# S5 mixer start-up: the scan's tables crossed over two PSUM banks, powers as three rows, x by channel half, and another order of GpSimd's work

## The chip, the cores and the metric

One core of a Trainium2 chip runs the whole program: a two-layer network on one sequence of 256 tokens, width 2048, in fp32. The metric is the device time of one execution in microseconds (us). The engines are TensorE (PE, matmuls and transposes through the identity), VectorE (DVE), ScalarE (ACT), GpSimd (POOL) and SyncE (SP, which here only issues DMAs). Each has its own instruction queue and runs it in order; between engines, and where one instruction of an engine needs an earlier one of the same engine, semaphores are waited on. PSUM, where PE writes its results, has eight banks of 512 fp32 values a partition.

## The reference, cut to what matters

Layer 0 is a mixer of diagonal state-space models ("S5"): 128 groups of 16 channels, 64 complex states a group. The state follows h[t] = lam * h[t-1] + B u[t], with lam = exp(dt * (a_re + i a_im)), and the output is Re(C h) plus a skip term, then gelu and a gated projection (GLU) with residual. Then comes a SwiGLU block, then layer 1 (dilated attention over three groups) and a second SwiGLU block. Cut to the mixer:

```
dt = exp(log_dt);  lb = exp(min(a_re, -1e-4)*dt) * (cos(a_im*dt) + i sin(a_im*dt))
coef = (lb - 1) / a;           bb = coef * b
bu = einsum('blgh,gph->blgp', u, bb)             # complex: _re and _im apart
st[t] = lb * st[t-1] + bu[t]                     # associative_scan in chunks of 128
y = einsum('blgp,ghp->blgh', st_re, c_re) - einsum('blgp,ghp->blgh', st_im, c_im) + d_skip*u
g = gelu(y);  val, gate = split(g @ w_glu);  x = x + val * sigmoid(gate)
```

## The kernel before, in words

The mixer does not scan 256 tokens. It takes four tokens as one step (so 64 steps, NS): the input of one step is the four tokens' inputs weighted with lam^3, lam^2, lam and 1 ("taps"), the step's factor is lam^4, and the outputs inside a step come from C lam^t ("fds", `powers`) and a small matrix over the four tokens ("mt", `build_m`). The 128 groups lie as 2 x 64 in partitions, and four quarters `qr` of 16 columns; a quarter has one chain of 63 steps.

All mixer work is issued through `InOrder` wrappers (T, A, G, W for PE, ACT, POOL, DVE), so that each engine's order is the order of the program text from line 547 on. The steps the change and the prediction touch:

- Lines 213-233: x as `xc` (two loads of 1 MB, on ACT's queue), `spp` (the state's parameters), `pairs`, `gb` and `bt` (gain and B), `ct` (C) on SP's.
- Lines 278-329: DVE computes `lam` from `spp` in about fifty instructions of 64 elements. ACT sums squares of x, PE adds them over partitions and repeats `NW` matmuls to keep its clock up, POOL takes the root, ACT scales x (`scale_x`).
- `form` and `power` (344-365): each power of lam is laid out as a 2x2 table of (re, im) factors in PSUM by four copies on DVE; ACT keeps the tables in SBUF as `pf` (`keep`). lam^4 is `tb3`, in a bank of its own; it holds the factors of all four chains (`fsc`), and the products of all four (`prs`) share the bank of table 2 (`tb2`).
- `gain` puts gain times B into `gps[qr]`; `taps(qr)` multiplies it by the powers (two products and an add for each of three taps). Quarters 0 to 2 are on DVE, 3 on POOL.
- `build_u(h)`: 32 transposes of x on PE, eight masked evictions by ACT. `taps_T(i)` transposes four columns' taps, `inject(i)` makes sixteen passes of matmul of them with x, and ACT copies the result into the state array `sts`; four injections make a quarter.
- `scan(qr)`: a generator of three DVE instructions a step: the product of the factor table with the state (128x64, into PSUM), and two adds into the next state (128x32). `run` takes one instruction of each generator in turn; `steps(n, a, b)` runs n steps of two chains.
- `build_c`, `powers` on POOL (chunks of two products and an add). `build_m`: ACT masks C, PE multiplies, ACT copies, SP moves copies by DMA. `y_local` and `y_state(qr, .., c0, c1)`: the outputs on PE, the state's part in halves of 32 steps. `gelu` on ACT, `turn` and `low` split the result into high and low fp32r halves as the left operand of the GLU.
- From line 679: 28 slots (`feed`) of twelve 128x512 matmuls, the first half of the GLU's depth, with chains 2 and 3 between them on DVE: a slot's DVE work is one `wlo` subtraction (the weights' low half) and two, two or three steps of both chains (`BSTEPS`). At slot 25 the last steps and `y_state(2)`, `y_state(3)` follow. The rest of the network begins after these slots.

Of the kernel before, what the change touches and what calls it, by code (L numbers as in the profile page):

```python
# [12 lines left out]
FP32 = mybir.dt.float32  # L13
# [3 lines left out]
ALU = mybir.AluOpType  # L17
# [30 lines left out]
NW = 14  # L48
# [14 lines left out]
class Net:  # L63
# [141 lines left out]
    def s5_glu(self):  # L205
# [110 lines left out]
        lam = early.tile([P, 2, 64], FP32, name="lam")  # L316
# [14 lines left out]
        tb0 = self.ps_mm.tile([P, 2, 2, 2, 64], FP32, name="mm")  # L331
        gpa = self.ps_mm.tile([P, 2, 16, GI], FP32, name="mm")
        tb2 = self.ps_mm.tile([P, 512], FP32, name="mm")
        tb3 = self.ps_mm.tile([P, 2, 2, 64], FP32, name="mm")
        half = lambda t, m: t.rearrange("p (k r m) -> p k r m", k=2, r=2)
        tabs = [tb0[:, 0], tb0[:, 1], half(tb2[:, 0:256], 64), tb3]
        prs = [half(tb2[:, 256 + 64 * k:320 + 64 * k], 16) for k in range(4)]
        fsc = [tb3[:, :, :, 16 * k:16 * k + 16] for k in range(4)]
        gpb = early.tile([P, 2, 16, GI], FP32, name="gpb")
        gqt = late.tile([P, 2, 2, 16, GI], FP32, name="gq", tag="gm", bufs=2)  # L340
        gq = [gqt[:, k] for k in range(2)]
        pf = late.tile([P, 4, 2, 2, 64], FP32, name="pf")
# [8 lines left out]
        def keep(t0, t1):
            for t in range(t0, t1):
                A.copy(out=pf[:, t].rearrange("p k r m -> p r k m"), in_=tabs[t])

        form(0, lam)
        pw = [lam]

        def power():
            k = len(pw)
            z = early.tile([P, 2, 64], FP32, name=f"pw{k}")  # L360
            pr = early.tile([P, 2, 2, 64], FP32, name="pr")
            tt(pr, tabs[0], pw[-1].unsqueeze(1).broadcast_to([P, 2, 2, 64]), ALU.mult, W)
            tt(z, pr[:, :, 0], pr[:, :, 1], ALU.add, W)
            pw.append(z)
            form(k, z)

        cf = late.tile([P, 2, 2, 64], FP32, name="cform")

        def coefs():
            ni = lam[:, 1]  # L370
            stt(t1, lam[:, 0], -1.0, ca, ALU.add, ALU.mult)
            tt(t2, ni, cb_, ALU.mult)
            stt(t3, lam[:, 0], -1.0, cb_, ALU.add, ALU.mult)
            tt(t4, ni, ca, ALU.mult)
            tt(cf[:, 0, 0], t1, t2, ALU.add)
            tt(cf[:, 0, 1], t3, t4, ALU.subtract)
            ts(cf[:, 1, 1], cf[:, 0, 0], -1.0, None, ALU.mult)
            V.tensor_copy(out=cf[:, 1, 0], in_=cf[:, 0, 1])
# [682 lines left out]
```

## Time and profile before

| what | us |
|---|---|
| median of three runs | 2454.3 (2450.5 to 2454.6) |
| profiled execution, its own time | 2451.0 |
| its span | 2449.2 |
| PE busy / DVE busy / ACT busy / POOL busy in the span | 2385.8 / 1377.0 / 1088.8 / 122.7 |
| first GLU matmul | 121.58 |
| second half of `y_state(2)` | 216.81 |

The span runs from the first to the last instruction. Busy times are sums of instruction lengths and overlap between engines. In a timeline row stand the start, the length, the engine (SPq or ACTq is a DMA issue), the line, the operation and its tiles as output<-inputs, with buffer numbers left out: in the mixer every instruction shows L60, the line of the recording wrapper, so they are told apart by tile and shape. `mm`, `tr` and `ms` are PSUM tiles, `actr` is any of the large SBUF tiles (x, the transposed x, the states, the mt matrices), `gp` a quarter's taps, `gt` their transposes, `fpr`, `cp` and `fdx` POOL's products, C and its powers.

### The profile page before, as it was taken

What the parts mean: (1) busy time and instruction counts of PE and PEld (TensorE: products, weight loads), DVE (VectorE), ACT (ScalarE), POOL (GpSimd) and SP (SyncE); (2) the same over time, 40 slices, a digit from 0 to 9 for tenths busy, and PEclk for the clock granted to TensorE, in tenths of its full rate; (3) what the DMA queues carried; (4) which work ended last, traced back from release to release, by engine and by line L of the source; (5) the groups of instructions that cost most, each with busy time, mean ns of one, the idle gap of its engine ahead of it and who ended that gap; (6) DMA issues with size and microseconds to landing.
All of it is one profiled execution on the core that took longest, in us unless ns stands there. A gap on an engine that the chain in (4) does not pass through costs nothing.

```text
span 2449.2 us, 29727 instructions
## 1 busy us (share of the span) xinstructions
PE 2385.8 (97%) x11856; PEld 1925.3 (79%) x11856; DVE 1377.0 (56%) x2309; ACT 1088.8 (44%) x1384; POOL 122.7 (5%) x105
## 2 busy tenths in 40 slices
PE   5689999999999999999999999999999999999999
PEld 4667887888888888888888888888878888888887
DVE  8897654544444445555546766775454444454444
ACT  6343554444334444454445555554443433344433
POOL 7600000000000000000000000000000000000000
PEclk8899999999999999999999999999999999999999
DMA  2244555555555555555554444445555555555554
GB/s 84 79 160 138 181 180 189 178 185 187 189 189 186 178 187 189 173 198 180 181 189 172 155 155 155 155 155 176 185 189 182 180 187 189 189 183 180 187 198 146
DMA packets 63036, 423.61 MB, mean 173 GB/s; under 512 B 8112, under 2 KB 9520, under 8 KB 12336
## 3 DMA queue, kind: packets, MB, share of 16 engines
q1 hardware_dynamic: 61456, 417.50, 49.9%
q10 hardware_dynamic: 1440, 4.19, 0.4%
q8 instruction: 93, 1.52, 0.2%
q14 instruction: 47, 0.39, 0.0%
HBM read 418.79 MB, written 2.10 MB: 172 GB/s over the span
## 4 chain that ended last, share of the span: by engine, by line
PE 91%; DVE 8%; issue 1%; ACT 0%; DMA 0%; DVEq 0%
PE mm L123 29%; PE mm L124 29%; PE mm L125 29%; DVE mm L60 3%; DVE actr L60 2%; DVE wlo L60 1%; PE ms L898 1%; PE tr L778 1%; PE tr L849 1%; PE tr L898 0%; PE tr L186 0%; PE tr L60 0%; PE mm L60 0%; DVE gp L60 0%; PE ms L60 0%
## 5 line engine op out<-in xcount | busy, mean ns | idle before, releaser
L105 DVE TENSOR_TENSOR wlo<-raw,whi 128x1024 fp32r<-128x1024 f32 x756 | 924.3, 1224 | 967.2 <-ACT whi L104 965.8
L104 ACT CAST whi<-raw 128x1024 fp32r<-128x1024 f32 x756 | 792.8, 1049 | 1125.7 <-PE mm L125 1102.0
L123 PE MATMUL mm<-whi,actt 128*128 128x512 f32 x3008 | 1196.8, 398 | 0.0
L124 PE MATMUL mm<-wlo,actt 128*128 128x512 f32 x3008 | 1190.9, 396 | 0.0
L125 PE MATMUL mm<-whi,actt 128*128 128x512 f32 x3008 | 1190.8, 396 | 0.0
L125 PEld LDWEIGHTS mm<-whi,actt 128*128 128x128 f32 x3008 | 564.7, 188 | 135.1
L123 PEld LDWEIGHTS mm<-whi,actt 128*128 128x128 f32 x3008 | 564.7, 188 | 132.9
L124 PEld LDWEIGHTS mm<-wlo,actt 128*128 128x128 f32 x3008 | 564.7, 188 | 132.5
L60 DVE TENSOR_TENSOR actr<-actr,mm 128x32 f32<-128x32 f32 x504 | 64.6, 184 | 8.0 <-ACT actr L60 3.5
L60 DVE TENSOR_TENSOR mm<-mm,actr 128x64 f32<-128x64 f32 x252 | 58.3, 231 | 8.1 <-ACT pf L60 0.4
L175 POOL TENSOR_TENSOR r<-m,mhalf 128x1 f32<-128x1 f32 x6 | 3.2, 552 | 1084.2 <-DVE m L174 846.7
L829 POOL TENSOR_TENSOR sc<-ssq,mhalf 128x8 f32<-128x8 f32 x16 | 32.1, 2004 | 474.9 <-DVE ssq L827 474.9
L60 ACT CAST whi<-raw 128x1024 fp32r<-128x1024 f32 x28 | 29.4, 1052 | 41.6 <-PE tr L60 21.0
L60 PE MATMUL tr<-whi,actt 128*128 128x512 f32 x128 | 42.1, 400 | 0.6 <-DVE actt L60 0.4
L764 ACT ACTIVATE sg<-mm,r 128x512 f32<-128x512 f32 x44 | 30.1, 688 | 21.3 <-PE mm L125 21.0
L907 ACT ACTIVATE s<-s,mx 128x384 f32<-128x384 f32 (+1 forms) x32 | 24.8, 774 | 29.1 <-DVE mx L905 29.1
L60 DVE TENSOR_TENSOR wlo<-raw,whi 128x1024 fp32r<-128x1024 f32 x28 | 34.1, 1221 | 0.0
L60 POOL TENSOR_TENSOR fpr<-pf,cp 128x512 f32<-128x512 f32 x32 | 33.2, 1059 | 1.2
L60 PE MATMUL tr<-wlo,actt 128*128 128x512 f32 x64 | 26.3, 412 | 5.2 <-DVE wlo L60 4.6
L768 DVE SCALAR_TENSOR_TENSOR sg<-mm,r,sg 128x512 f32<-128x512 f32 x44 | 30.9, 743 | 0.2 <-issue 0.2
L60 PE MATMUL mm<-whi,actt 128*128 128x512 f32 x96 | 30.7, 396 | 0.0
L825 ACT ACTIVATE sq<-mm 128x512 f32<-128x512 f32 x32 | 19.0, 593 | 23.5 <-PE mm L125 23.5
(202 smaller groups left out, 1101.9 us busy)
## 6 DMA issues: line engine op xcount, KB each, us to landing
raw<-w_gu SPq DMA_DIRECT2D x176, 1024.0 KB, 4.8
raw<-w_down SPq DMA_DIRECT2D x88, 1024.0 KB, 4.8
raw<-w_q SPq DMA_DIRECT2D x48, 1024.0 KB, 4.8
raw<-w_glu SPq DMA_DIRECT2D x32, 1024.0 KB, 4.9
raw<-w_kv SPq DMA_DIRECT2D x32, 1024.0 KB, 4.7
raw<-w_o SPq DMA_DIRECT2D x16, 1024.0 KB, 4.8
actr<-x_c ACTq DMA_DIRECT2D x2, 1024.0 KB, 7.2
xr<-x_t SPq DMA_DIRECT2D x8, 256.0 KB, 5.2
```

The source lines that it names most:

```text
L60: return lambda *a, **k: self.tc.keep_in_program_order(call(*a, **k))
L104: (scalar or self.nc.scalar).copy(out=hi, in_=r)
L105: (vector or self.nc.vector).tensor_tensor(out=lo, in0=r, in1=hi.bitcast(FP32), op=ALU.subtract)
L123: matmul(ps[th], lhsT=a[:, 0, ts], rhs=hi, start=(k == k0), stop=False)
L124: matmul(ps[th], lhsT=a[:, 0, ts], rhs=lo, start=False, stop=False)
L125: matmul(ps[th], lhsT=a[:, 1, ts], rhs=hi, start=False, stop=(k == n - 1))
L764: nc.scalar.activation(out=s, in_=ps[th], func=AF.Silu, scale=rs[th])
L768: nc.vector.scalar_tensor_tensor(out=sg[th], in0=ps[th], scalar=rs[th], in1=sg[th], op0=ALU.mult, op1=ALU.mult)
L778: nc.tensor.transpose(out=pt[:, k, th * P:(th + 1) * P], in_=sg[th][:, c:c + P], identity=self.ident)
L829: nc.gpsimd.tensor_tensor(out=sc, in0=ssq, in1=self.mhalf.rearrange("p (a b) -> p a b", a=2), op=ALU.pow)
L849: nc.tensor.transpose(out=pt[:, hh, th * P:(th + 1) * P], in_=ns[th][:, 2 * hp + hh], identity=self.ident)
L907: nc.scalar.activation(out=sc, in_=sc, func=AF.Exp, scale=SM_SCALE, bias=mx, accum_out=z)
```

## The change

- **Tables.** `form` and its four copies a power go. The powers lie in SBUF as `pz`, three rows each (-im, re, im), so that both columns of the 2x2 table are two neighbouring rows; ACT copies the first three powers to PSUM (`tab`, `tab3`). All three products are now computed before the first taps, by `ts`, `tt` on DVE. POOL reads `pz` where it read `pf`, and C's factor is three rows too.
- **Banks.** Of two PSUM banks, `bp` holds `tab3`, the factors of chains 0 and 2 and the products of chains 1 and 3; `bq` holds the factors of chains 1 and 3, the products of chains 0 and 2, and is also the second buffer of tap products. ACT writes the factors of chains 0 and 2, DVE those of 1 and 3 (`table`).
- **Scan order.** A chain runs `LEAD` = 5 steps and one instruction ahead of its partner: 0 before 1, then 2 before 3; the end of chain 1 runs beside the start of chain 2.
- **Taps** of quarters 0 and 1 alternate two pairs of product buffers, in an order with an add behind a product of the next tap.
- **x** is laid out by channel half, so `scale_x(0)` and `build_u(0)` need half of it; its loads go to SP's queue behind `spp`. `build_u` groups its evictions by half as well. An injection is copied by one ACT instruction.
- **Order.** POOL does C's first chunk before the gains; `scale_x(1)` and `build_m(0)` come before `build_u(1)`; POOL's `powers` come later in the text. `turn(0)` comes before the second half of `y_state(1)`. `NW` falls from 14 to 8.

DVE, where chains 0 and 1 begin to run together (numbers tell the tiles apart: `mm_240` factors, `mm_239` products of both chains and table 2, `gp2` and `gpb` taps, `actr_107` the states). Before:

```order
L60 TENSOR_TENSOR mm_239<-mm_240,actr_107 128x64
L60 TENSOR_TENSOR mm_238<-mm_239,gp2_251 128x512
L60 TENSOR_TENSOR actr_107<-actr_107,mm_239 128x32
L60 TENSOR_TENSOR gpb_241<-mm_239,gp2_251 128x512
L60 TENSOR_TENSOR actr_107<-actr_107,mm_239 128x32
L60 TENSOR_TENSOR gp2_251<-mm_238,gpb_241 128x32x16
L60 TENSOR_TENSOR mm_239<-mm_240,actr_107 128x64 x2
L60 TENSOR_TENSOR actr_107<-actr_107,mm_239 128x32 x4
```

The same place now (`mm_234` is `bp`, `mm_235` is `bq`):

```order
L61 TENSOR_TENSOR mm_235<-mm_234,actr_107 128x64
L61 TENSOR_TENSOR actr_107<-actr_107,mm_235 128x32
L61 TENSOR_TENSOR mm_234<-mm_235,actr_107 128x64
L61 TENSOR_TENSOR actr_107<-actr_107,mm_235 128x32
L61 TENSOR_TENSOR actr_107<-actr_107,mm_234 128x32
L61 TENSOR_TENSOR mm_235<-mm_234,actr_107 128x64
```

Products and adds of both chains stood in pairs, all through `mm_239`; now the two chains are half a step apart, and an instruction and its neighbour belong to different chains.

ACT, from the last injection of chain 1 to the first transposed taps of chain 2 (`actr_108` transposed x, `actr_85` x, `actr_109` the mt matrices). Before:

```order
L60 COPY actr_107<-ms_565 128x2x2x63 x2
L60 COPY actr_107<-ms_576 128x2x2x63 x2
L60 ACTIVATE actr_108<-tr_587,masks_97 128x8x64 x2
L60 ACTIVATE actr_108<-tr_598,masks_97 128x8x64 x2
L60 ACTIVATE actr_108<-ms_609,masks_97 128x8x64 x2
L60 ACTIVATE actr_108<-ms_620,masks_97 128x8x64 x2
L60 COPY gt_631<-tr_632 128x512
```

Now:

```order
L61 COPY actr_107<-ms_513 128x2x4x63
L61 ACTIVATE actr_85<-actr_85,rc_135 128x32x16 x4
L61 ACTIVATE cb_527<-cp_244,masks_97 128x8x32 x2
L61 ACTIVATE cb_530<-cp_244,masks_97 128x8x32 x2
L61 COPY actr_109<-ms_533 64x256 x2
L61 ACTIVATE actr_108<-tr_560,masks_97 128x8x64 x2
L61 ACTIVATE actr_108<-tr_561,masks_97 128x8x64 x2
L61 ACTIVATE actr_108<-ms_582,masks_97 128x8x64 x2
L61 ACTIVATE actr_108<-ms_583,masks_97 128x8x64 x2
L61 COPY gt_604<-tr_605 128x512
```

The second half of x is scaled here, and `build_m(0)` (`cb`, then `actr_109`) stands before the evictions.

The diff, cut:

```diff
-NW = 14
+NW = 8
+LEAD = 5
...
-        for q in range(2):
-            A.dma_start(out=xc[:, 16 * q:16 * q + 16], in_=io["x_c"][:, 16 * q:16 * q + 16])
         spp = early.tile([P, 3, 64], FP32, name="spp")
         nc.sync.dma_start(out=spp, in_=io["sp"])
+        for q in range(2):
+            nc.sync.dma_start(out=xc[:, 16 * q:16 * q + 16], in_=io["x_c"][:, 16 * q:16 * q + 16])
...
+        ts(pz[:, 0, 0], pz[:, 0, 2], -1.0, None, ALU.mult)
+        tab = self.ps_mm.tile([P, 2, 3, 64], FP32, name="mm")
+        ga = [self.ps_mm.tile([P, 512], FP32, name="mm")]
+        bp, bq = [self.ps_mm.tile([P, 512], FP32, name="mm") for _ in range(2)]
+        ga.append(bq)
...
+        tab3 = bp[:, 256:448].rearrange("p (z m) -> p z m", z=3)
+        tabs = [tab[:, 0], tab[:, 1], tab3]
+        cut = lambda t, a: t[:, a:a + 128].rearrange("p (q k r m) -> p q k r m", q=2, k=2, r=2)
+        fp, prq, fq, prp = cut(bp, 0), cut(bq, 0), cut(bq, 128), cut(bp, 128)
+        fsc = [fp[:, 0], fq[:, 0], fp[:, 1], fq[:, 1]]
+        prs = [prq[:, 0], prp[:, 0], prq[:, 1], prp[:, 1]]
+        def power(t):
             pr = early.tile([P, 2, 2, 64], FP32, name="pr")
+            for r in range(2):
+                tt(pr[:, r], pz[:, 0, 1 - r:3 - r], pz[:, t - 1, 1 + r].unsqueeze(1).broadcast_to([P, 2, 64]), ALU.mult)
+            tt(pz[:, t, 1:3], pr[:, 0], pr[:, 1], ALU.add)
+            ts(pz[:, t, 0], pz[:, t, 2], -1.0, None, ALU.mult)
...
+            seq = "m20 m21 m10 a2 m11 m00 a1 m01 a0" if two else "m20 m21 a2 m10 m11 a1 m00 m01 a0"
...
-            for j in range(2):
-                m0 = 4 * j2 + 2 * j
-                A.copy(out=st[:, 1:64, :, m0:m0 + 2].rearrange("p c r m -> p r m c"),
-                       in_=ps[:, j, :, :, 0:63])
+            A.copy(out=st[:, 1:64, :, 4 * j2:4 * j2 + 4].rearrange("p c r m -> p r m c"), in_=ps[:, :, :, 0:63])
...
         coefs()
-        power()
-        power()
+        for t in range(1, 4):
+            power(t)
         gain(0, W)
-        for qr in (1, 3, 2):
+        scale_x(0)
+        A.copy(out=tab, in_=pz[:, 0:2])
+        A.copy(out=tab3, in_=pz[:, 2])
+        build_u(0)
+        table(fp, 0, A)
+        build_c(0)
+        for qr in (1, 2, 3):
             gain(qr, G)
         run(taps(0))
-        for h in range(2):
-            scale_x(h)
-        build_u(0)
-        keep(0, 3)
-        build_c(0)
+        run(taps(1))
+        d_skip()
+        taps_g(3)
         build_c(1)
...
+        table(fq, 1, W)
+        third = taps(2, False)
+        run(itertools.islice(third, 4))
+        run(itertools.islice(sq[0], 3 * LEAD + 1), third)
         for i in range(4, 7):
             g0, gtt = gtt, taps_T(i + 1)
             inject(i, g0)
         inject(7, gtt)
+        scale_x(1)
+        build_m(0)
         build_u(1)
...
-        steps(28, sq[0], sq[1])
+        steps(62 - 32 - LEAD, sq[0], sq[1])
+        run(itertools.islice(sq[0], 2), itertools.islice(sq[1], 3))
...
-        steps(3, sq[1], sq[2])
+        pts = [turn(0, j4) for j4 in range(2)]
+        run(itertools.islice(sq[1], 1))
+        run(sq[1], itertools.islice(sq[2], 3 * LEAD))
...
-        pts = [turn(0, j4) for j4 in range(2)]
...
+        run(itertools.islice(sq[2], 1))
...
+            if k == len(slots) - 3:
+                run(sq[2], itertools.islice(sq[3], 3))
```

More of the change, by code (lines that the diff above doesn't have):

```diff
@@ L351, in keep @@
[L351 to L360, printed above, removed]
-            pr = early.tile([P, 2, 2, 64], FP32, name="pr")
[L362 to L365, printed above, removed]
@@ L367, in s5_glu @@
-        cf = late.tile([P, 2, 2, 64], FP32, name="cform")
+        ts(pz[:, 0, 0], pz[:, 0, 2], -1.0, None, ALU.mult)
[3 more added lines that the diff above has]
+        ga.append(bq)
+        ga = [t.rearrange("p (k m i) -> p k m i", k=2, i=GI) for t in ga]
+        gpb = [early.tile([P, 2, 16, GI], FP32, name=f"gpb{k}") for k in range(2)]
@@ L369, in coefs, with table @@
+        def table(out, par, eng):
+            src = pz[:, 3].rearrange("p z (q e m) -> p z q e m", q=2, e=2)
+            for r in range(2):
+                o, i = out[:, :, :, r].rearrange("p q k m -> p k q m"), src[:, 1 - r:3 - r, :, par]
+                if eng is A:
+                    A.copy(out=o, in_=i)
+                else:
+                    eng.tensor_copy(out=o, in_=i)
+        cf = late.tile([P, 3, 64], FP32, name="cform")
         def coefs():
@@ L405, in taps @@
-        def taps(qr, eng=None):
+                        src = xc[64 * y:64 * y + 64, 16 * h + 8 * g + j].rearrange("p x s i -> p (x s i)")
+                        T.transpose(out=pss[y][:, j], in_=src,
+                                    identity=self.ident[64 * y:64 * y + 64, 64 * y:64 * y + 64])
+                for y in range(2):
+                    for xx in range(2):
+                        A.activation(out=ub[h][:, 8 * g:8 * g + 8, y, xx], in_=pss[y], func=AF.Copy,
+                                     scale=masks[:, xx:xx + 1])
@@ L455, in build_c @@
             mo = 16 * qr
-            pair(cp[:, :, mo:mo + 16], cf[:, :, :, mo:mo + 16], ct[:, :, mo:mo + 16])
+            pair(cp[:, :, mo:mo + 16], [cf[:, k:k + 2, mo:mo + 16] for k in range(2)], ct[:, :, mo:mo + 16])
         def m_operand(qr, j4):
@@ L513, in powers @@
             for t in range(4):
-                pair(fds[qr][:, t], pf[:, t, :, :, mo:mo + 16], cp[:, :, mo:mo + 16])
+                pair(fds[qr][:, t], [pz[:, t, 1 - k:3 - k, mo:mo + 16] for k in range(2)], cp[:, :, mo:mo + 16])
         def y_local(qr, pool, nm):
@@ L567, in s5_glu @@
             inject(i, g0)
-            if i == 0:
-                keep(3, 4)
-        fds = {qr: self.xres.tile([P, 4, 2, 16, GI], FP32, name="fdx", tag="xr") for qr in range(1)}
-        powers(0)
-        build_c(2)
-        build_c(3)
-        fds[1] = self.xres.tile([P, 4, 2, 16, GI], FP32, name="fdx", tag="xr")
-        powers(1)
-        sq = [scan(qr) for qr in range(4)]
-        run(itertools.islice(sq[0], 9), taps(2))
+        table(fq, 1, W)
+        third = taps(2, False)
+        run(itertools.islice(third, 4))
+        run(itertools.islice(sq[0], 3 * LEAD + 1), third)
         for i in range(4, 7):
```

90 lines of the change are left out of this document (41 added, 49 removed).

## The prediction

> **What bounds the kernel now.** I read the windows first: only the first 240 us differ from one long run of matmuls, and the diff ends there. Then the timeline, for what TensorE (PE) waits for at the two ends of the scan.
>
> ```profile
> 114.77 3.45 PE L60 MATMUL tr<-fdx,actr 64*32 64x64 f32 x128 [14.60 <-DVE actr L60]
> 121.58 0.50 PE L60 MATMUL tr<-whi,actt 128*128 128x512 f32 x1 [0.26 <-ACT actt L60]
> 121.58:216.81 95.23, 83.40 (x513) 61.80 (x513) 88.78 (x393) 38.81 (x50) 0.00 (x0) 1.00 0.47 160
> 216.81 3.60 PE L60 MATMUL ms<-actr 64*32 64x64 f32 x128 [2.27 <-DVE actr L60]
> ```
>
> In a timeline row stand start, length, instruction, and in brackets the idle time and its releaser. In the windows row (third) the length is followed by the busy time of PE, weight loads, VectorE (DVE), ScalarE (ACT) and GpSimd. PE stood idle 14.6 us for the first scan pair, began the GLU at 121.58, then ran it with chains 2 and 3 beside it (DVE busy 88.8 of 95.2), and stood idle for DVE again at 216.81. So in stage 1 (to 121.58) and stage 2 (to 216.81) the scan on DVE sets the end; behind that PE does, and nothing there is edited.
>
> One step of both chains, from narrow windows of the timeline (a row with x2 starts with the first of the two):
>
> ```profile
> 59.97 0.23 DVE L60 TENSOR_TENSOR mm<-mm,actr 128x64 f32<-128x64 f32 x1
> 60.24 0.23 DVE L60 TENSOR_TENSOR mm<-mm,actr 128x64 f32<-128x64 f32 x1
> 60.51 0.19 DVE L60 TENSOR_TENSOR actr<-actr,mm 128x32 f32<-128x32 f32 x1
> 60.61 0.30 DVE L60 TENSOR_TENSOR actr<-actr,mm 128x32 f32<-128x32 f32 x2
> 60.73 0.29 DVE L60 TENSOR_TENSOR actr<-actr,mm 128x32 f32<-128x32 f32 x2
> 60.83 0.18 DVE L60 TENSOR_TENSOR actr<-actr,mm 128x32 f32<-128x32 f32 x1
> 61.05 0.23 DVE L60 TENSOR_TENSOR mm<-mm,actr 128x64 f32<-128x64 f32 x1
> ```
>
> The order is product A, product B, adds A, B, A, B: 1.076 us a pair. Adds start 0.10 to 0.12 apart though each lasts 0.18 to 0.19, so neighbours overlap. But product B starts 0.27 behind product A, which is A's length and 0.04 more, though it needs nothing of A; the first add again 0.27 behind B; and the next product A 0.22 behind the last add of B. These three are full waits for the neighbour. Is it the bank? The place where scan 0 runs between the tap products answers:
>
> ```profile
> 45.86 0.22 DVE L60 TENSOR_TENSOR mm<-mm,actr 128x64 f32<-128x64 f32 x1
> 45.99 0.69 DVE L60 TENSOR_TENSOR mm<-mm,gp 128x512 f32<-128x512 f32 x1
> 48.01 0.22 DVE L60 TENSOR_TENSOR mm<-mm,actr 128x64 f32<-128x64 f32 x1
> 48.27 0.70 DVE L60 TENSOR_TENSOR mm<-mm,gp 128x512 f32<-128x512 f32 x1
> ```
>
> Both times an unrelated product follows a scan product. At 45.99 it reads `tabs[1]`, another bank, and starts 0.13 later. At 48.27 it reads `tabs[2]`, which shares its bank with the scan products: 0.26.
>
> **The change part by part: the scan.** Factors and products now lie crossed in two banks and chain A runs ahead, so the order is product A, add B, add A, product B, add A, add B, and an instruction needs only the one two places before it. From the rows: behind a product the next instruction may start after 0.13, behind an add after 0.10; a result is usable 0.26 behind a product's start and 0.22 behind an add's. Chain 3 alone, at the end, shows these latencies without neighbours:
>
> ```profile
> 216.89 0.23 DVE L60 TENSOR_TENSOR mm<-mm,actr 128x64 f32<-128x64 f32 x1
> 218.30 0.23 DVE L60 TENSOR_TENSOR mm<-mm,actr 128x64 f32<-128x64 f32 x1
> ```
>
> Two steps in 1.41, so 0.705 = 0.26 + 0.22 + 0.22 each. That is the floor of a pair; the issue distances add to 2 x 0.13 + 4 x 0.10 = 0.66. Laid out one after the other (0, 0.13, 0.26, 0.36, 0.49, 0.62, then 0.72) I get 0.72 to 0.74; I take 0.73 instead of 1.076.
>
> **The beginning.**
>
> ```profile
> spp<-sp SPq DMA_DIRECT2D x1, 96.0 KB, 4.6
> actr<-actr SPq DMA_DIRECT2D x8, 48.0 KB, 2.0
> ct<-c SPq DMA_DIRECT2D x1, 1024.0 KB, 9.2
> 14.50 0.23 DVE L248 TENSOR_TENSOR lam<-t,mag 128x64 f32<-128x64 f32 x1
> 14.66 3.82 POOL L60 TENSOR_TENSOR gp<-bt,gb 128x512 f32<-128x512 f32 x3
> 14.72 5.01 ACT L60 ACTIVATE actr<-actr,rc 128x512 f32<-128x512 f32 x8 [1.30 <-POOL rc L60]
> 14.77 1.30 DVE L248 TENSOR_TENSOR t<-lam,cb__224 128x64 f32<-128x64 f32 x1
> 23.89 1.59 DVE L60 TENSOR_TENSOR gp<-bt,gb 128x512 f32<-128x512 f32 x1
> 25.51 0.70 DVE L60 TENSOR_TENSOR mm<-mm,gp 128x512 f32<-128x512 f32 x1
> 26.12 0.68 DVE L60 TENSOR_TENSOR gpb<-mm,gp 128x512 f32<-128x512 f32 x1
> 44.43 0.19 DVE L60 TENSOR_TENSOR actr<-actr,mm 128x32 f32<-128x32 f32 x1 [3.50 <-ACT actr L60]
> ```
>
> `spp` took 4.6 us beside x; issued ahead of x on one queue, it is bounded by 2.0 (a small transfer with nothing beside it) and 4.6; nearer the first, so it lands 2.2 earlier. The decay is then there at 12.3 instead of 14.5. `gb` and `bt` were there by 14.66, where GpSimd used them, and the same bytes now only go in another order; `ct` waits for a landing before its issue, as before, and is there near 16. The stalls against GpSimd (1.30 instead of 0.22 at 14.77, 1.59 instead of 0.70 at 23.89) go, but the first chunk of C still starts on GpSimd as soon as its factor and `ct` are there, not strictly behind the powers, and can catch `gain(0)`: I leave 0.9 in. Coefficients and three powers, now 22 small instructions at 0.1 to 0.3, take 4.1; `gain(0)` ends at 12.3 + 4.1 + 0.7 + 0.9 = 18.0 instead of 25.5. Tap products come each 0.61 (26.12 - 25.51), nine for a quarter. A new wait stands in them: `tab3` shares a bank with the factor copies on ACT, and those are queued on ACT behind the scaling of x (at 13.6, 1.1 earlier with x ahead on the queue; four of 5.01 / 8, so to 16.1), two copies, the transposes and the eight evictions of `build_u(0)` (0.61 each: 2.46 / 4 at 50.07, below), to 22.7 in all; the sixth tap instruction would be ready at 21.0, so 1.7 is lost, and everything behind it on DVE with it. Quarter 0 is done at 25.2.
>
> **The chain on PE and ACT.** What the scan waits for, and what becomes the bound:
>
> ```profile
> 31.77 1.94 PE L60 MATMUL tr<-ident,gp 128*128 128x128 f32 x8 [10.45 <-DVE gp L60]
> 42.21 1.09 PE L60 MATMUL ms<-actr,gt 128*64 128x128 f32 x16
> 43.82 1.09 PE L60 MATMUL ms<-actr,gt 128*64 128x128 f32 x16
> 50.07 2.46 ACT L60 ACTIVATE actr<-tr,masks 128x512 f32<-128x512 f32 x4
> 54.62 1.19 ACT L60 COPY gt<-tr 128x512 f32<-128x512 f32 x2
> 69.60 1.69 ACT L60 ACTIVATE cb<-cp,masks 128x256 f32<-128x256 f32 x4
> 75.16 1.71 ACT L60 ACTIVATE cb<-cp,masks 128x256 f32<-128x256 f32 x4
> 93.86 2.28 PE L60 MATMUL tr<-fdx,actr 64*32 64x64 f32 x128
> ```
>
> The transposes of quarter 0 started at 31.77, so they start 6.5 earlier. An injection costs 1.61 on PE (43.82 - 42.21); one copy instead of two takes nothing from that, and costs nothing. With the slow first two (1.94 for eight transposes) injection 3 is copied at 35.1 instead of 44.4, injection 7 near 41.2. Chain 0 has five steps by then, and 58 pairs follow: 41.2 + 58 x 0.73 = 83.5 instead of 114.77.
>
> But PE and ACT are not ready then. `scale_x(1)` (four activations of 0.62, 2.5) and `build_m(0)` (75.16 - 69.60 = 5.6) now stand ahead of `build_u(1)` (54.62 - 50.07 = 4.6): the copy that was at 54.62 comes at 41.2 + 2.5 + 5.6 + 4.6 = 53.9, hardly earlier. From there to the first y_state it was 39.2, now without `build_m(0)` 33.7: 87.6, 6 earlier. The two first halves (2.1 each, and the 1.8 that was lost between them) and the second half of quarter 0 (2.2) end near 96; `gelu`, transposes and, now ahead of the GLU, `y_state(1)` add 4.1: GLU at 100.2, 21.3 earlier. Hidden in this: the DVE half (83.5), the first weight load (behind `build_m(2)`, as before), and GpSimd, whose list is only reordered. At 1.27 an instruction at most (3.82 / 3 at 14.66) a chunk of three is 3.8; up to the second set of factors there are sixteen chunks and the skip term: from 16 to at most 79, before `y_state(1)` at 90. Without that cover each microsecond it is late is one on the path. The six warm-up matmuls less, the layout of x and the powers as three rows are covered by the same waits.
>
> **Stage 2.**
>
> ```profile
> 139.54 1.22 DVE L60 TENSOR_TENSOR wlo<-raw,whi 128x1024 fp32r<-128x1024 f32 x1
> 150.12 1.22 DVE L60 TENSOR_TENSOR wlo<-raw,whi 128x1024 fp32r<-128x1024 f32 x1
> 235.31 0.39 PE L123 MATMUL tr<-whi,actt 128*128 128x512 f32 x1
> 238.11 0.39 PE L123 MATMUL tr<-whi,actt 128*128 128x512 f32 x1
> ```
>
> Three slots (2, 2 and 3 pairs) took 10.58; less 7 x 0.346 that is 8.2, 2.7 a slot. A slot's twelve matmuls take 238.11 - 235.31 = 2.80: PE becomes the bound. 26 slots are 72.8; the transposes, `y_local(2)` and the first half of `y_state(2)` among them add 5.4, and I leave 2 for two engines so evenly matched: 80 instead of 95.2, 15 less. Sum: 21.3 + 15 = 36.
>
> **Rivals.** *The wait is not the bank's.* The pair stays at 1.076. Then 41.2 + 58 x 1.076 = 103.6 instead of 114.8, 0.7 lost to the moved `y_state(1)`, stage 2 as it is: 10.5 less, 2441. Against it stands 45.99 beside 48.27; for it, that these are one instance each. *The chain gives less.* PE and ACT start y_state at 93.9 as before, and PE still waits 0.3 a slot for `wlo`: 6 + 8 less gain, 2429. For it: 53.9 against 54.62, and the two rates in stage 2. *Overlap is lost* (the slower side): now every scan instruction carries a wait, and if each must see its neighbour finished, a pair costs 2 x 0.23 + 4 x 0.185 = 1.20, and with 0.04 of release each 1.42. Both stages hold 118 pairs, and the earlier start pays up to a pair of 1.165; at 1.20 the time is 2455, at 1.42 (+8.8, +0.7, +20.6) it is 2481. Against it: the add at 60.73 waits for the one at 60.51 and yet starts while the one at 60.61 runs.
>
> By the Trainium skill (VectorE: DVE Perf Modes, The DRAIN you can't avoid) the next Vector instruction does not start until the pipe is empty, wait or no wait. By that rule the pair would be this last rival's 1.20. The trace differs: 0.10 between adds that last 0.19.
>
> **How the numbers follow.** The profiled execution took 2451.0 (span 2449.2 and 1.8 around it); less 36 is 2415. The median of the runs, 2454.3, lies 3.3 above it, two of three there; I say 2417. Chances: forecast 0.62, chain 0.22, bank 0.08, lost overlap 0.08 (half of it at 1.20, which is +0.17% and so no change). Forecast's own range 2407 to 2424 (spp 0 to 2.6, pair 0.705 to 0.8, stage 2 at 78 to 84); to hold 8 in 10 it reaches over the chain's case and to the edge of the bank's: 2406 to 2438. About 0.2% (5 us) can be told from no change: faster 0.92, same 0.04, slower 0.04.
>
> **What would show it.** A pair of 0.73 between successive products of one chain; no DVE row over 0.7 between the decay and the taps but `gain(0)`; an ACT wait inside quarter 0's taps; the first y_state released by ACT or PE and not by DVE; GLU near 100; slots of 2.8 to 2.9 without waits for `wlo`; `y_state(2)` near 180. A pair over 1.1, or a GLU later than 112, would prove it wrong.

## The result, and the profile after

The changed kernel takes 2423.9 us (median of four runs, 2422.6 to 2425.1), the kernel before 2453.1 beside it (2450.5 to 2454.6): a ratio of 0.9882, 95% interval 0.9865 to 0.9899. That is 29 us less, where 36 were forecast: inside the range, and 7 us above the point. The profiled execution took 2423.3 (before: 2451.0), 27.7 less. I follow the forecast along this trace.

The stretch that the prediction called stage 2, from the first GLU matmul to the second half of `y_state(2)`, in the windows view of the changed kernel:

```profile
109.21:189.01 79.80, 78.74 (x517) 63.27 (x512) 74.84 (x390) 36.70 (x46) 0.00 (x0) 1.00 0.54 186
```

79.8 us instead of 95.2, and PE is busy in 78.7 of them: PE is the bound there now. The GLU begins at 109.21 instead of 121.58. So 15.4 came from stage 2 and 12.4 from its earlier start, 27.8 together: behind it nothing else moved. Forecast were 15 and 21.3. The whole gap lies ahead of 109.21.

The scan itself, two chains running together (narrow window of the timeline, DVE; a row with x2 starts with the first of the two):

```profile
60.02 0.23 DVE L61 TENSOR_TENSOR mm<-mm,actr 128x64 f32<-128x64 f32 x1
60.15 0.32 DVE L61 TENSOR_TENSOR actr<-actr,mm 128x32 f32<-128x32 f32 x2
60.38 0.23 DVE L61 TENSOR_TENSOR mm<-mm,actr 128x64 f32<-128x64 f32 x1
...
60.74 0.23 DVE L61 TENSOR_TENSOR mm<-mm,actr 128x64 f32<-128x64 f32 x1
```

Product A at 60.02, product B at 60.38, product A at 60.74: a pair takes 0.72 to 0.73, where it took 1.076. An add now starts 0.13 behind a product that is 0.23 long.

The beginning (timelines of DVE, POOL and PE):

```profile
12.31 0.23 DVE L249 TENSOR_TENSOR pz<-t,mag 128x64 f32<-128x64 f32 x1
15.52 0.48 DVE L249 TENSOR_TENSOR pr<-pz 128x128 f32<-128x128 f32 x2
16.47 0.69 DVE L61 TENSOR_TENSOR gp<-bt,gb 128x512 f32<-128x512 f32 x1
22.31 0.70 DVE L61 TENSOR_TENSOR mm<-mm,gp 128x512 f32<-128x512 f32 x1 [1.96 <-ACT mm L61]
...
16.75 2.34 POOL L61 TENSOR_TENSOR fpr<-cform,ct 128x512 f32<-128x512 f32 x2 [2.96 <-DMA ct<-c]
...
25.07 1.94 PE L61 MATMUL tr<-ident,gp 128*128 128x128 f32 x8 [7.42 <-DVE gp L61]
```

The decay is there at 12.31, `gain(0)` takes 0.69 at 16.47, the new wait for ScalarE stands in the taps with 1.96, and the transposes of quarter 0 start at 25.07 instead of 31.77. GpSimd starts its first chunk at 16.75, 0.2 behind the end of the last power and 0.28 behind the start of `gain(0)`: it had waited 2.96 for C to land. That small margin comes back in an experiment below.

Then the two places where the time is missing. First PE and ScalarE between the halves of the injections (timelines):

```profile
40.69 2.54 ACT L61 ACTIVATE actr<-actr,rc 128x512 f32<-128x512 f32 x4
...
56.82 1.12 ACT L61 COPY gt<-tr 128x512 f32<-128x512 f32 x2
...
44.08 7.09 PE L61 MATMUL ms<-cb,gp 128*128 128x64 f32 x32 [3.02 <-ACT cb L61]
57.51 1.97 PE L61 MATMUL ms<-actr,gt 128*64 128x128 f32 x16 [1.67 <-ACT gt L61]
```

and the windows view of the same place (the last but two numbers is the granted clock):

```profile
44.08:51.17 7.09, 7.09 (x34) 6.97 (x36) 7.09 (x60) 0.75 (x2) 6.78 (x7) 0.50 0.00 1
51.17:60.00 8.83, 6.67 (x60) 5.35 (x60) 8.83 (x74) 6.89 (x13) 8.44 (x9) 0.50 0.08 23
```

`scale_x(1)` and the masking of C keep PE idle for 3.02, the granted clock falls from 1.00 (36 to 41) to 0.50, and the 32 matmuls of `build_m(0)`, which took 3.7 to 3.8 at the other three places, take 7.09. The clock stays at 0.50 to about 63; on the way PE waits for ScalarE twice more, 0.44 before 53.57 and 1.67 before 57.51. Second, the state products (PE's timeline):

```profile
90.74 2.30 PE L61 MATMUL tr<-fdx,actr 64*32 64x64 f32 x128
92.83 1.11 PE L61 MATMUL mm<-fdx,actr 64*32 64x64 f32 x50
96.24 1.25 PE L61 MATMUL mm<-fdx,actr 64*32 64x64 f32 x69 [2.31 <-issue]
...
101.62 2.36 PE L61 MATMUL tr<-fdx,actr 64*32 64x64 f32 x78 [2.71 <-issue]
104.71 1.97 PE L61 MATMUL ms<-ident,gm 128*128 128x128 f32 x8 [0.74 <-ACT gm L61]
109.21 0.50 PE L61 MATMUL tr<-whi,actt 128*128 128x512 f32 x1
```

In 384 small matmuls PE stops twice, for 2.31 and 2.71, and the releaser is "issue": no wait that the profile shows. The DMA view of a window of 2 us around the first stop (93.0 to 95.0; queue, kind, transfers, MB, share) has this:

```profile
q8 instruction: 1, 0.02, 3.0%
```

One transfer of 16 KB on the instruction queue. In the whole execution this queue has 92 of them, and PE has 11844 matmuls and as many weight loads: 257 instructions a transfer. In the trace this one runs from 93.92 to 94.86, and PE goes on at 96.24, 1.38 behind its end. At the second stop it ends at 100.11 and PE goes on 1.51 behind. Between the two stops PE issues 128 matmuls (78 and 50), and with their weight loads that is 256 instructions. The transposes at 104.71 take 1.97 instead of 1.03, again at half clock behind the idle time.

### The profile page after: what moved, and what is told of

Same layout as the page of the kernel before. It is cut to its first block, busy times and chain, and to the rows that moved or that the text cites. A ratio compares the mean times of both kernels' runs of the same rounds, so it can differ in the third digit from the quotient of the medians.

```text
span 2420.8 us, 29676 instructions
## 1 busy us (share of the span) xinstructions
PE 2383.9 (98%) x11844; PEld 1927.5 (80%) x11844; DVE 1344.8 (56%) x2301; ACT 1088.9 (45%) x1368; POOL 124.4 (5%) x105
## 3 DMA queue, kind: packets, MB, share of 16 engines
q8 instruction: 92, 1.51, 0.2%
## 4 chain that ended last, share of the span: by engine, by line
PE 98%; ACT 1%; issue 0%; DVE 0%; DMA 0%; POOL 0%; SPq 0%; DVEq 0%; POOLq 0%; ACTq 0%
PE mm L124 29%; PE mm L125 29%; PE mm L126 29%; PE tr L61 2%; PE ms L61 2%; PE mm L61 2%; PE ms L917 1%; PE tr L797 1%; ACT actr L61 1%; PE tr L868 1%; PE tr L917 0%; PE tr L187 0%; DMA actr<-x_c 0%; PE ms L947 0%; PE tr L125 0%
## 5 line engine op out<-in xcount | busy, mean ns | idle before, releaser
L61 DVE TENSOR_TENSOR actr<-actr,mm 128x32 f32<-128x32 f32 x504 | 81.0, 183 | 1.4 <-ACT actr L61 0.6
L783 ACT ACTIVATE sg<-mm,r 128x512 f32<-128x512 f32 x44 | 30.1, 688 | 21.3 <-PE mm L126 21.0
L61 POOL TENSOR_TENSOR fpr<-pz,cp 128x512 f32<-128x512 f32 x32 | 35.0, 1116 | 1.3
L61 ACT COPY actr<-ms 128x504 f32<-128x504 f32 (+1 forms) x24 | 19.7, 823 | 23.8 <-PE ms L61 22.5
```

What stands on the lines that cost most here:

```text
L61: return lambda *a, **k: self.tc.keep_in_program_order(call(*a, **k))
L783: nc.scalar.activation(out=s, in_=ps[th], func=AF.Silu, scale=rs[th])
```

## Experiments on what is missing

The kernel before was run beside every group of experiments: its medians were 2453.8, 2453.1 and 2452.4, and 2453.1 beside the change. So a difference between medians of two groups holds to about 1 us.

**One pass of state products.** The stops might be a limit of the instruction supply, or come from the weights that are being loaded at that time.

```
-        for qr in range(2):
-            y_state(qr, yl[qr], 0, 32)
...
-        y_state(0, yl[0], 32, 64)   # and y_state(1, ..) the same
+        y_state(0, yl[0], 0, 64)
```

> The change with one edit: the state products of quarters 0 and 1 are issued once over all 64 chunk positions instead of twice over 32, so 256 matmuls of 64x32 weights become 128 and 128 become 0 in each place (512 small PE instructions fewer). My theory: in the changed kernel PE stood idle 2.31 and 2.71 us (releaser 'issue') because it ran out of fetched instructions inside these bursts: each stop came 166 to 178 small matmuls into a burst, and PE ran on 1.4 us behind the end of a 16 KB transfer on the instruction queue. With one pass both stops go; ScalarE's weight casts then hold the first gelu to 96.5, and the first GLU matmul comes near 101.5 instead of 109.2: the time is 7 to 8 us less, 2416. Rival: the stops come from the DMA traffic of the first GLU weights (DMA share 0.70 at 90 to 100): then a stop of 2 us or more stays in front of or inside the single pass, and the gain is only the 2.2 us per pass that is not issued, 4 at most, 2420. If the stop was no loss on the path, 2424.

Measured: 2416.8 us (2416.3 to 2418.4), 7.2 less than the change. PE's timeline:

```profile
91.47 4.26 PE L61 MATMUL tr<-fdx,actr 64*64 64x64 f32 x128
...
99.60 4.21 PE L61 MATMUL mm<-fdx,actr 64*64 64x64 f32 x128
103.74 0.51 PE L61 MATMUL tr<-whi,actt 128*128 128x512 f32 x1
```

No stop is left in these passes. A pass with 64x64 weights takes 4.2, as long as two with 64x32 (2.3 and 2.2), so the work is not less; what went is the stops, and I had wrongly expected that it would also save 2.2 a pass (GLU at 103.7 and not 101.5).

**The same stops without the weights' DMA.** A copy of the first gelu's result into each weight buffer keeps the loads back; for this the second half of quarter 0's state products and its gelu are issued ahead of the weight casts:

```
+                if k < 6:
+                    A.copy(out=raws[b, c][:, 0, 0:16], in_=gms[0][:, 0, 0, 0, 0])
...
+        y_state(0, yl[0], 32, 64)
+        gms[0] = gelu(yl[0])
         high(0)
         high(1)
-        y_state(0, yl[0], 32, 64)
-        gms[0] = gelu(yl[0])
```

> The change with the first loads of the GLU weights held back until the first gelu is done (a small copy of its result into each weight buffer ahead of the load). It asks only whether those loads cause PE's stops between the state products (2.31 and 2.71 us in the changed kernel). If the loads cause them by keeping the DMA engines busy, the stops shrink to under 1 us in all. If PE simply runs the small instructions faster than 16 KB of them are fetched, at least 2 us of stops stay. The first GLU matmul comes later in any case, near 111, with a time of 2424 to 2428, which says nothing.

Measured: 2432.6 (one run). PE's timeline, and the windows of this kernel and then of the changed one over the same stretch (last three numbers: clock, DMA share, GB/s):

```profile
94.97 1.26 PE L61 MATMUL mm<-fdx,actr 64*32 64x64 f32 x69 [1.15 <-issue]
98.97 1.45 PE L61 MATMUL tr<-fdx,actr 64*32 64x64 f32 x78 [1.85 <-issue]
```

```profile
92.00:99.00 7.00, 4.00 (x246) 3.71 (x237) 0.00 (x0) 1.07 (x2) 6.69 (x7) 1.00 0.13 33
```

```profile
92.00:99.00 7.00, 4.60 (x245) 4.22 (x236) 3.43 (x2) 3.11 (x4) 6.76 (x6) 0.89 0.64 204
```

With the DMA share at 0.13 instead of 0.64 the stops are 3.0 instead of 5.0, so they do not need that traffic, and the larger part is the supply of instructions itself. What the traffic adds is not settled: with the loads in place the same bursts stop for 3.7 to 6.7 in the profiled executions of other kernels (2.05 and 1.65 in the uncrossed one below, 3.35 and 3.30 with x first). That the supply ends the stops is inferred from the 256 instructions between them and from the transfer that ends just ahead; no view names it. 128 small matmuls with their weight loads are 256 instructions, so one transfer, and take 2.3 us. The Trainium skill (Runtime: NRT & Kernel Launch, Instruction fetch mechanics) says that instructions come in blocks of 16 KiB, 256 instructions, and that the cost of crossing into the next is mostly hidden. The block agrees with the trace; that it is hidden does not hold for such bursts: 1.15 us (this kernel) to 2.71 (the change) a stop.

**The clock.** Two kernels take the 3.02 us gap away in different ways. One moves the scaling to where ScalarE was idle (22.3 to 26.2 in the changed kernel), so that PE also starts earlier:

```
         table(fp, 0, A)
+        scale_x(1)
...
-        scale_x(1)
         build_m(0)
```

> The change with one edit: the scaling of the second half of x (four ScalarE activations, 2.54 us) stands right behind the factor copies at 22.3, where ScalarE was idle for 3.9 us, instead of ahead of build_m(0). My theory: PE was idle 3.0 us at 41.0 to 44.1 for it, the granted clock fell to 0.5 from 42 to 63, and the 32 matmuls of build_m(0) took 7.09 instead of 3.79. Without the 2.54 the gap is about 0.6, build_m(0) starts near 41.7 and takes 3.8, the second half of the injections runs at 1.09 an injection throughout, and the first state product comes at 83 to 85 instead of 90.74; the time is 5 to 7 us less, 2418. Rival: the clock is not the cause of the 7.09; then only the 2.5 us of waiting goes, first state product at 88, 2421. Second rival: the chain on PE and ScalarE is not what the GLU waits for, 2424.

The other fills the gap with unused matmuls and moves nothing:

```
+        self.warm(14, pairs, T)
         scale_x(1)
         build_m(0)
```

> The change with 14 unused 128x128 matmuls (about 3 us at full clock) on PE ahead of build_m(0), which fill the 3.0 us gap at 41.0; nothing else is moved. It separates the clock from the wait. My theory: the clock stays at full speed, build_m(0) takes 3.8 instead of 7.09 though it starts no earlier than 44.0, the injections behind build_u(1) take 1.09 instead of 1.98, and the first state product comes 4 to 5 us earlier, near 86; the time is 3 to 5 us less, 2420. Rival, the clock is not the cause: build_m(0) keeps its 7 us, time 2424.

Measured: 2417.5 (2414.5 to 2418.3) with the scaling moved, 2418.3 (2416.6 to 2418.9) with the gap filled. PE's timeline of the first, then of the second:

```profile
41.31 3.79 PE L61 MATMUL ms<-cb,gp 128*128 128x64 f32 x32 [0.55 <-ACT cb L61]
51.18 1.97 PE L61 MATMUL ms<-actr,gt 128*64 128x128 f32 x16 [2.13 <-ACT gt L61]
```

```profile
39.66 3.39 PE L61 MATMUL tr<-pairs 128*128 128x128 f32 x28
44.02 3.79 PE L61 MATMUL ms<-cb,gp 128*128 128x64 f32 x32
88.03 2.28 PE L61 MATMUL tr<-fdx,actr 64*32 64x64 f32 x128
103.77 0.50 PE L61 MATMUL tr<-whi,actt 128*128 128x512 f32 x1
```

In the second, `build_m(0)` starts where it started in the changed kernel, 44.02 against 44.08, and takes 3.79 at a granted clock of 1.00 instead of 7.09 at 0.50. So its length was the clock's; the 14 useless matmuls (28 in the trace) save 5.7 us. In both kernels the first two injections behind `build_u(1)` still take 1.97, which I had expected to go: idle pieces of 0.6, 0.5 and 2.1 stand ahead of them, and the clock falls to 0.50 at the beginning of the last in one kernel (49.3) and in the middle of it in the other (52.9). The GLU starts 5.4 earlier in the second although the first state product is only 2.7 earlier: ahead of the first gelu the stops for instructions were shorter in that execution (1.28 and 1.55; a third of 1.82 came behind the transposes), and the last burst and the transposes ran at full clock. How long the stops are differs between executions; the next experiment's kernel, with the same order of PE's instructions as the change, stopped for 2.05 and 1.65 and began its GLU at 106.67.

## Experiments on the scan

Are the waits the bank's, and what are crossing and order worth? Four kernels change only the tiles or the order of the scan. **Uncrossed**, each chain with factors and products in one bank of its own:

```
-        prs = [prq[:, 0], prp[:, 0], prq[:, 1], prp[:, 1]]
+        prs = [prp[:, 0], prq[:, 0], prp[:, 1], prq[:, 1]]
```

> The change with the two banks uncrossed: each chain has its factors and its products in one bank, and the two chains in different banks. The order of instructions and the distance of every wait are the same (two places back). If what matters is on which earlier instruction each one waits, a pair stays at 0.73 and the time at 2424 within 0.2%. If crossing itself is needed, because an instruction that reads and writes one bank is slower, the product takes longer than its 0.23 and a pair comes to 0.8 or more: 2.95 or more a slot in stage 2, 2428 or more.

Measured: 2423.2 (2419.9 to 2425.0), the pair 0.73:

```profile
59.85 0.23 DVE L61 TENSOR_TENSOR mm<-mm,actr 128x64 f32<-128x64 f32 x1
...
60.58 0.23 DVE L61 TENSOR_TENSOR mm<-mm,actr 128x64 f32<-128x64 f32 x1
```

Crossing does nothing of its own. Two banks are enough, whichever way they are dealt out, as long as an instruction need not wait for its neighbour.

**One bank, same order**, and **two banks, chains side by side**, and **one bank and side by side**, as before the change:

```
-        fp, prq, fq, prp = cut(bp, 0), cut(bq, 0), cut(bq, 128), cut(bp, 128)
+        fp, fq = cut(bp, 0), cut(bp, 128)                                # one bank
+        pra, prb = [bp[:, a:a + 64].rearrange(..) for a in (448, 256)]
...
-        prs = [prq[:, 0], prp[:, 0], prq[:, 1], prp[:, 1]]
+        prs = [pra, prb, pra, prb]
...
-        run(itertools.islice(sq[0], 3 * LEAD + 1), third)                # side by side
+        run(itertools.islice(sq[0], 3 * LEAD), third)
...
```

> The change with the factors of all chains and the products of both running chains in one bank; order and lead are the same. By the bank theory each product then waits for the add just ahead of it (0.22), the add behind a product for that product though it is the other chain's (0.27), and the second add follows at 0.10: a pair is 2 x 0.59 = 1.18 instead of 0.73. Stage 1: chain 0 ends near 41.3 + 58 x 1.18 = 110 instead of 83, the second half of the state product waits for it again, GLU near 117 instead of 109; stage 2: three slots take 7 x 1.18 + 3.05 on VectorE, 3.77 a slot instead of 2.80, 23 more; the time is about 2455, no better than before the change. Rival, it is the order with its lead that gives the gain and not the banks: the pair stays under 0.85 and the time under 2431.

> The change with its banks, but the two chains without the offset of one instruction: product A, product B, add A, add B, add A, add B. Then product B reads its factors in the bank into which product A has just written, and waits 0.27 for it; the adds of B wait for product B in turn. Laid out: 0, 0.27, 0.40, 0.53, 0.63, 0.75, next product 0.85. By the bank theory a pair is 0.85 and 2.8 to 3.0 us a slot become 3.0 in stage 2, 5 us in all: 2429. If only the banks count and not the order, 0.73 and 2424; if the order is all, near 1.076 and 2441 or more.

> The change with all factors and products of the scan in one bank and the two chains side by side, as they ran before the change; all other edits are kept. It prices the scan's part of the change alone. Bank theory: product B waits for product A (0.27), the first add for product B (0.27), then 0.10, 0.12, 0.10 and 0.22: a pair of 1.08, as before the change. Chain 0 ends near 41.3 + 58 x 1.08 = 104, GLU near 111.5; stage 2 as before, 95: the time is 2441, the number that the first rival of the prediction gave for a pair of 1.076. Rival: the other edits alone give nearly all of the gain, 2430 or less.

Measured, in this order: 2451.8 (2451.0 to 2453.2), 2424.3 (2423.3 to 2427.1), 2437.4 (2436.7 to 2438.9). The DVE timelines, one fence a kernel:

```profile
59.99 0.28 DVE L61 TENSOR_TENSOR actr<-actr,mm 128x32 f32<-128x32 f32 x2
60.31 0.23 DVE L61 TENSOR_TENSOR mm<-mm,actr 128x64 f32<-128x64 f32 x1
...
61.16 0.28 DVE L61 TENSOR_TENSOR actr<-actr,mm 128x32 f32<-128x32 f32 x2
```

```profile
60.32 0.49 DVE L61 TENSOR_TENSOR mm<-mm,actr 128x64 f32<-128x64 f32 x2
61.17 0.49 DVE L61 TENSOR_TENSOR mm<-mm,actr 128x64 f32<-128x64 f32 x2
```

```profile
59.94 0.50 DVE L61 TENSOR_TENSOR mm<-mm,actr 128x64 f32<-128x64 f32 x2
61.01 0.50 DVE L61 TENSOR_TENSOR mm<-mm,actr 128x64 f32<-128x64 f32 x2
```

Pairs of 1.17, 0.85 and 1.07, where 1.18, 0.85 and 1.08 were worked out. The sum of issue distance and latency holds to 0.01 in all five arrangements; the last of them repeats the arrangement from which most of the terms were read. What sets the wait, a semaphore of the program or the chip, no view here shows: the runs show that it follows the bank, and that it lasts as long as a wait for the whole earlier instruction would. Their times say what the scan's part of the change is worth. With the pair as before (one bank, side by side) and all other edits, 15.7 of the 29.2 us are still gained (15.0 against the kernel before in its own group); the scan gives the other 13.5 to 14.2. And the new order is no good by itself: in one bank it makes the pair longer than before, and the whole gain is gone (ratio to before 0.9997, interval 0.9988 to 1.0006).

The second of the three leaves something open. A pair of 0.85 should have cost 5 us in stage 2; in its profiled execution stage 2 took 83.1 instead of 79.8 (GLU at 110.71, second half of `y_state(2)` at 193.79), but the median of its runs is only 0.4 above that of the change, and the profiled run is the longest of its four. What 0.12 a pair costs here is between nothing and 4 us.

## An experiment on the beginning

What is the earlier decay worth? x goes back to ScalarE's queue, beside the parameters:

```
+        for q in range(2):
+            A.dma_start(out=xc[:, 16 * q:16 * q + 16], in_=io["x_c"][..])
         spp = early.tile([P, 3, 64], FP32, name="spp")
         nc.sync.dma_start(out=spp, in_=io["sp"])
-        for q in range(2):
-            nc.sync.dma_start(out=xc[..], in_=io["x_c"][..])
```

> The change with one edit undone: x is again loaded from ScalarE's queue beside the state parameters on SP's queue, instead of behind them on one queue. By my sum the decay then comes 2.2 later (14.5 instead of 12.3), and with it the taps of quarter 0, all injections, the PE and ScalarE chain and the GLU: 2426. Rival: the beginning is not on the path, or x comes earlier by as much as the parameters come later: 2424.

Measured: 2431.4 (2429.2 to 2434.1), 7.4 more and not 2.2. The timelines of DVE, POOL and PE:

```profile
14.47 0.23 DVE L249 TENSOR_TENSOR pz<-t,mag 128x64 f32<-128x64 f32 x1
15.77 1.36 DVE L249 TENSOR_TENSOR pr<-pz 128x128 f32<-128x128 f32 x2
18.23 1.21 DVE L241 TENSOR_SCALAR pz<-pz 128x64 f32<-128x64 f32 x1
...
15.92 2.13 POOL L61 TENSOR_TENSOR fpr<-cform,ct 128x512 f32<-128x512 f32 x2 [1.10 <-DVE cform L241]
...
33.28 1.94 PE L61 MATMUL tr<-ident,gp 128*128 128x128 f32 x8 [14.42 <-DVE gp L61]
```

The decay is 2.2 later, as worked out. But C has now landed before the powers begin, so GpSimd starts at 15.92, 0.15 behind the first of them, and each small power instruction waits for a large GpSimd one: the two products take 1.36 instead of 0.48, a negation of 64 elements 1.21 instead of 0.20. The powers last from 15.8 to 26.8 instead of 13.6 to 16.6, and quarter 0 comes 8.2 later. The Trainium skill (SBUF — State Buffer, Who interferes with whom) says so: a VectorE instruction with two SBUF inputs, or in a two-port mode, and a GpSimd instruction that reads SBUF shut each other out for a whole instruction. This trace agrees: most instructions of 0.2 to 0.3 take 0.7 to 2.0. In the changed kernel nothing keeps GpSimd behind the powers but the late landing of C.

## What follows from them, in one kernel

The two losses should add up. This kernel takes the state products in one pass, scales x early, splits `build_u(1)` around `build_m(0)` so that PE has no gap near 50, and puts the first gelu ahead of the second weight cast:

```
         table(fp, 0, A)
+        scale_x(1)
...
-        scale_x(1)
-        build_m(0)
-        build_u(1)
-        gtt = taps_T(8)
+        cb0 = [m_operand(0, j4) for j4 in range(2)]
+        build_u(1, [0])
+        ahead = []
+        build_m(0, cb0, lambda: ahead.append(taps_T(8)))
+        build_u(1, [1])
+        gtt = ahead[0]
...
```

> What the first four runs point to, in one kernel: the state products of quarters 0 and 1 in one pass each; the second half of x scaled where ScalarE is idle at 22.3; the transposes and evictions of build_u(1) split, one half ahead of build_m(0) and one behind it, with the transposes of quarter 2 begun before the second half, so that PE has no gap of 2 us around 50; the first gelu ahead of the second weight cast. My theory: the two losses are separate and add up. First state product at 81 to 84 instead of 90.74, then bounded by chain 0, which ends near 83.5; two passes of 4.2, gelu, transposes: first GLU matmul at 94 to 97 instead of 109.2; stage 2 as it is at 80; time 2409 to 2412. Rival: something else is late next (the weights, which landed at 94.5, or the low halves on VectorE), GLU at 100 or later, 2415.

Measured: 2407.7 (2407.0 to 2408.7), ratio to before 0.9819 (0.9804 to 0.9833).

```profile
82.96 4.18 PE L61 MATMUL tr<-fdx,actr 64*64 64x64 f32 x128 [2.81 <-DVE actr L61]
93.94 0.51 PE L61 MATMUL tr<-whi,actt 128*128 128x512 f32 x1
```

PE is ready at 80.2 and waits for the scan again, which ends near 82.9, where the prediction had put it at 83.5, and the GLU starts at 93.9. From here two more edits. Chain 0's factor copies go ahead of `build_u(0)`, against the wait of 1.96 in the taps:

```
+        table(fp, 0, A)
         build_u(0)
-        table(fp, 0, A)
```

> The combined kernel with the factor copies of chain 0 and 2 (0.53 on ScalarE) ahead of build_u(0) instead of behind its eight evictions. The wait of 1.96 inside the taps of quarter 0 (releaser ScalarE, the bank that tab3 shares with the factors) goes; transposes, injections and the scan start 1.4 to 1.9 earlier. In the combined kernel the first state product waited for chain 0, so this comes through to the GLU: 92 to 92.5 instead of 93.94, time 2406. Rival: PE is late instead (it was at 80.2 in front of the state product, and moves with it) or the low halves are: 2408.

And, upon that, the first pass of quarter 0 again by itself, in PE's idle time:

```
+        y_state(0, yl[0], 0, 32)      # ahead of the weights
-        y_state(0, yl[0], 0, 64)
+        y_state(0, yl[0], 32, 64)
```

> The kernel of the run before with the state product of quarter 0 again in two passes (quarter 1 stays in one): the first pass fits into the 2.8 us in which PE waits for chain 0, the second takes 2.3 instead of 4.2 behind it. If a stop for fetching comes only when the fetched block is used up faster than the next arrives, the idle time between the passes covers the fetch and the GLU comes 1.5 to 1.9 earlier: time 2404. Rival: 128 small matmuls more bring a stop of 1.5 to 2.7 back into the second pass or the transposes behind it, and the gain is gone: 2406 to 2407.

Measured: 2405.2 (2404.9 to 2407.2) for the first, ratio 0.9810 (0.9797 to 0.9823), 18.8 less than the change and the lowest of all, though its interval overlaps that of the combined kernel; 2410.6 (2408.6 to 2412.1) for the second, 5.4 worse. PE's timeline of the first, then of the second:

```profile
81.14 4.12 PE L61 MATMUL tr<-fdx,actr 64*64 64x64 f32 x128 [1.36 <-DVE actr L61]
91.29 0.50 PE L61 MATMUL tr<-whi,actt 128*128 128x512 f32 x1
```

```profile
81.79 1.09 PE L61 MATMUL tr<-fdx,actr 64*32 64x64 f32 x51 [0.47 <-DVE actr L61]
84.83 1.44 PE L61 MATMUL tr<-fdx,actr 64*32 64x64 f32 x77 [1.96 <-issue]
91.50 2.95 PE L61 MATMUL mm<-fdx,actr 64*64 64x64 f32 x86 [0.94 <-issue]
94.38 0.79 PE L61 MATMUL tr<-whi,actt 128*128 128x512 f32 x1
```

With 128 small matmuls more the stops are back, 1.96 and 0.94, though PE had stood idle ahead of the second pass: 0.47 of idle time does not cover a fetch. The rival that I had written down for this kernel was right in its mechanism; at 2406 to 2407 it had put the cost some 4 us too low. In the first kernel the wait of 1.96 is gone, but not all of it is gained: GpSimd there starts at 16.38, ahead of `gain(0)` at 16.47, which takes 1.55 instead of 0.69, and quarter 0 is done at 23.7 instead of 24.9.

## Why the prediction was right or wrong

| step | forecast | trace of the change |
|---|---|---|
| decay there | 12.3 | 12.31 |
| `gain(0)` ends | 18.0 | 17.2 |
| new wait in the taps | 1.7 | 1.96 |
| taps of quarter 0 done | 25.2 | 24.9 |
| injections 3 and 7 copied | 35.1, 41.2 | 35.0, 40.9 |
| pair of steps | 0.73 | 0.73 |
| chain 0 done | 83.5 | 82.6 (its last add starts at 82.39) |
| copy ahead of the second injections | 53.9 | 56.8 |
| first state product | 87.6 | 90.74 |
| second half of quarter 0 done | near 96 | 103.98 |
| first GLU matmul | 100.2 | 109.21 |
| stage 2 | 80 | 79.80 |

- **The scan**: right in its mechanism and its size. Three false waits between neighbours, for a shared bank, made the pair; five arrangements of banks and order gave the pairs that the distances 0.13 and 0.10 and the latencies 0.26 and 0.22 give.
- **The beginning**: right to a few tenths. The 0.9 that I left for a collision of `gain(0)` with GpSimd did not come in this execution, by a margin of 0.28. It is real: in three other profiled executions `gain(0)` took 1.55 to 1.59 instead of 0.69 (the kernel with the scaling moved and the last two). It would have been hidden here, since the taps wait for ScalarE up to 22.3 in any case: with the scaling moved, `gain(0)` ended 1.8 later than in the change, and quarter 0 was done at 24.7, no later. What I had not seen is the larger collision, with the powers: with x first they lasted 11.1 instead of 3.0.
- **Stage 2**: right, bound by PE.
- **The chain on PE and ACT** is the step that failed, in two terms. "`build_m(0)` 5.6" was read from rows at full clock (75.16 - 69.60) and put into a place where PE would have just stood idle for the scaling of x; I had counted that wait, 2.5, and not what it does to the clock. It cost 2.9 up to the copy, 3.1 up to the first state product. The other term is "the 1.8 that was lost between them": I took a stop that the profile of before shows once, with the releaser "issue", as it stood there, and moved a third burst of the same small matmuls right behind the two. The stops became 5.0, 3.2 more, and the last pass ran at half clock behind them (78 matmuls in 2.36, where 128 take 2.3), so 4.8 were added there; the transposes at half clock and what hangs on them added 1.0. With the 3.1 that makes the 9.0 by which the GLU was late. One pass instead of two gives 7.2 of the time back, a gap moved or filled 6.5 and 5.7, which shows both. That the time still fell inside the range is no merit of this part: it stands at the edge of the forecast's own range (2407 to 2424).
- "Hidden in this: the DVE half (83.5)" was right, and is why the faster scan gave only some 14 us: up to the GLU PE was late, not DVE. Only with PE's two losses removed does the scan set the end of stage 1 again.
- **The rivals**: "The chain gives less" is the one that came nearest: its 2429 lies 5 us from the measured time, the forecast's 2417 lies 7. But its mechanism is not the one: it took 6 from the start because PE and ScalarE would begin the state products at 93.9 (it was 90.74, half of that), and 8 from stage 2 for waits for `wlo`, which did not come; the rest was lost in the state products. "The wait is not the bank's" is out by the pair, and its 2441 is 3.6 more than what a pair of 1.07 does cost (2437.4). "Overlap is lost" is out: the add at 60.15 starts 0.13 behind a product that takes 0.23, so the next VectorE instruction does not wait here for its neighbour's end. The section of the Trainium skill that the prediction cites beside this rival (VectorE: DVE Perf Modes, The DRAIN you can't avoid) also says that a next operation which is not held starts earlier; I had left that out, and this trace fits it.

## What to carry to other kernels

Where instructions of one engine share a PSUM bank, count for each on which earlier instruction it has to wait: an order that puts every wait two places back, over two banks, brought the pair from 1.076 to 0.73, and the same order in one bank made it 1.17. When a step is moved to where its engine has just been idle, price it at the clock that the idle time leaves (7.09 against 3.79 here), and fill the gap or move what makes it. A stop with the releaser "issue" in a burst of small matmuls is a cost that came again 256 instructions later: look for fewer, larger ones before anything is added to the burst.

## What the runs showed of the hardware that I had not expected

- PE ran 128 matmuls with their weight loads (64x32 weights, 64 columns) in 2.3 us and then stopped; the stops between these state products were 0.9 to 3.4, and PE went on 1.4 to 1.5 us behind the end of a 16 KB transfer of instructions (both stops of the change). With 64x64 weights, 4.2 us a burst, there was none ahead of the GLU, except the 0.94 of the last kernel, right behind two bursts of the small ones. Larger weights are no full cure: in the state products behind stage 2, bursts with 128x64 and 64x64 weights (128 of them in 4.4 us) stopped for 0.2 to 0.7 in most of the kernels.
- An idle gap of 3.0 us was followed by 21 us at half clock, with gaps of 0.4 to 1.7 inside them (the clock fell after 1.7 us of the gap); 3.4 us of useless matmuls in the gap were worth 5.7.
- VectorE instructions of 0.2 to 0.3 us took up to 2.0 while GpSimd worked through SBUF: 2.2 us of lateness ahead of them became 8.2 behind them.
